# Which element-wise steps stand behind a read-out, and which engine takes the last unit's two subtractions, in the recurrence of a hybrid attention block

## The chip, the cores and the metric

The kernel runs on one core of a Trainium2 chip. The metric is the device time of one execution in microseconds; where several runs are given, their median. One further execution was profiled, and every duration below is from that profile or its trace.

## The reference

One block of a network on a sequence of 1024 positions with width 1024: a normalised and modulated input goes through one large projection `w_in`; its columns feed three things, an attention with a forget gate, a recurrence with a state for each of 8 heads, and two sigmoid gates that mix both results. A convolutional feed-forward part follows. What matters here is the recurrence:

```python
def step(state, inp):
    r_t, w_t, k_t, v_t, a_t, b_t = inp
    sa = jnp.einsum('bhvk,bhk->bhv', state, a_t)
    state = state * w_t[:, :, None, :] + sa[..., None] * b_t[:, :, None, :] + v_t[..., None] * k_t[:, :, None, :]
    y_t = jnp.einsum('bhvk,bhk->bhv', state, r_t)
    return state, y_t
...
mean = jnp.mean(y, axis=-1, keepdims=True)
var = jnp.mean(jnp.square(y - mean), axis=-1, keepdims=True)
y = ((y - mean) * lax.rsqrt(var + GN_EPS)).reshape(bsz, seq, RWKV_WIDTH) * ln_w + ln_b
```

It is computed in chunks of 64 positions, with matrices inside a chunk and a state handed from chunk to chunk.

## The kernel before, in words

**Stages.** Up to about 130 us come the modulation and the first projections; from about 140 to 610 us the recurrence; from 621 to 813 us the attention; after that the output projections and the feed-forward part, which is dense matrix work. All precise products are made from a higher half (`hi`, a rounded copy) and a lower half (`lo`, what the rounding left), in three passes.

**Units.** The recurrence works on eight units, numbered k = 0 to 7: four pairs of heads `p`, each in two halves `hf` of 512 positions. `pre(k, p, hf)` prepares a unit and `main(k, p, hf)` runs it. In `pre`, element-wise steps on VectorE (DVE) make the operands `ar` and `bk` and the product `rkb` (lines 780 to 792 of the kernel before); the matmuls `p` then multiply `bk` and `ar`, and their results are read into `E`. From `E` a triangular system goes through memory (`sm`, then `M`) and is solved on DVE by 31 pairs of small steps, `t` (line 828) and `E` (line 832); the result goes back through memory (`se`, then `TT`) to be used in `main` of that unit. The solving steps of one unit and the element-wise steps of the next are mixed in DVE's queue.

**The end of a unit.** `main` ends with a normalisation of `y` within each head. Its two sums over a head, `mu` and `va`, are made on TensorE (PE) by `head_sums`: ScalarE (ACT) rounds the input to a higher half (`Ztr`, `Zts`), GpSimd (POOL) subtracts to get the lower half (`Wtr`, `Wts`, line 735), and after a planned pause of 3400 ns two matmuls sum both halves.

**What fills PE.** Between the small matmuls of the recurrence, PE works through a queue of projection items: `ps_rkv` (inputs of later units), `v` (the values of the attention, in 16 pieces), and `gt` (gates). Each item fills one of two banks of the pool `pb` ("big"); it must be read out by ACT and DVE before the item after the next can begin in that bank. The read-out of `ps_rkv` is DVE line 410, that of `v` is line 1002 (`vs`). Both call `evac_done`.

**What sets the order.** PE's order is written by a planner (`Weave`): it adds up an estimate `weave.now` in ns for each matmul, and a chain that yields a number is taken up again when `weave.now` has moved on by it; until then PE gets projection items. DVE's, ACT's and POOL's order in this stage is made by a scheduler from the program and from added order dependences (`add_manual_dep`, without a semaphore). One such rule is the list `soft`: `evac_done(i)` puts each step in the list behind the read-out `i`, if the step was written less than 3000 planned ns before, and in the kernel before then empties the list.

**After the last unit.** `load_head(0)` and `load_head(1)` bring the attention's operands of the first two heads into `stA`, `stB` and `vh` by DMAs from POOL's queue; the attention's first matmuls are named `lg`.

Of the kernel before, what the change touches and what calls it, by code (L numbers as in the profile page):

```python
# [12 lines left out]
ALU = mybir.AluOpType  # L13
# [121 lines left out]
def hybrid_block(ctx: ExitStack, tc: tile.TileContext, a, out):  # L135
    nc = tc.nc
    weave = Weave()
    ctx.enter_context(tc.manual_schedule(engines={mybir.EngineType.PE}))

    def mm(o, lhsT, rhs, start, stop, more=False):  # L140

        weave.mm_cost(o, lhsT, rhs)
        nc.tensor.matmul(o, lhsT, rhs, start=start, stop=stop, skip_group_check=more)  # L143
# [5 lines left out]
    def f32(ap):  # L149
        return ap.bitcast(F32)  # L150

    tt, stt, ts = nc.vector.tensor_tensor, nc.vector.scalar_tensor_tensor, nc.vector.tensor_scalar
# [15 lines left out]
    def V(name, i=0, n=1):  # L168
        o, _ = VEC[name]
        return vec[:, o + i : o + i + n]  # L170
# [16 lines left out]
    nw0, na0, nkk, oka = (quads[:, 4 * x : 4 * x + 4] for x in range(4))  # L187
# [64 lines left out]
    soft = []  # L252

    def evac_done(i):
        for x, t in soft:
            if weave.now - t < 3000:
                tc.add_manual_dep(x.ins, i.ins.name, NOSYNC)
        soft.clear()
        return i
    first_step = []  # L260

# [8 lines left out]
    def behind_state(i):  # L270
        if marks.get("chain"):
            held.append(i)
        else:
            behind(i, "S")
# [112 lines left out]
    with ExitStack() as es:  # L387
# [7 lines left out]
        def gen(name):  # L395
            return pr.tile([128, NH], F32, tag="gen", name=name)

        def shifted(w, ti, hf, dst, prev, name, by_kt=False):

            ps = big(f"ps_{name}{hf}")  # L400
            yield from gemm_steps(ps, w, u, slice(hf * NH, hf * NH + NH), by_kt=by_kt)
            sh = shp.tile([128, NH + 1], F32, tag="sh", name=f"sh_{name}{hf}")
            if hf == 0:
                nc.vector.memset(sh[:, 0:1], 0.0)
            else:
                nc.vector.tensor_copy(sh[:, 0:1], prev)
            nc.scalar.activation(sh[:, 1 : NH + 1], ps, AF.Copy, scale=V("mu", ti))
            if hf == 0:
                nc.gpsimd.tensor_copy(prev, sh[:, NH : NH + 1])
            marks["bank"] = evac_done(stt(dst, ps, omu[:, ti : ti + 1], sh[:, 0:NH], op0=ALU.mult, op1=ALU.add))  # L410
# [16 lines left out]
        def qk_steps(w, i):  # L427
            sc_ = 0.125 if i < 4 else 1.0
            for hf in range(2):
                cs = slice(hf * NH, hf * NH + NH)  # L430
                ps = big(f"qk{i}_{hf}")
                yield from gemm_steps(ps, w, u, cs)
                hi = gsp.tile([128, NH], F32R, tag="sp0", name=f"qh{i}_{hf}")
                nc.scalar.activation(hi, ps, AF.Copy, scale=sc_)
                lo = gsp.tile([128, NH], F32R, tag="sp0", name=f"ql{i}_{hf}")
                evac_done(stt(lo, ps, sc_, f32(hi), op0=ALU.mult, op1=ALU.subtract))
                h0 = 2 * (i % 4)
                for t, k, r0 in ((hi, 0, 0), (lo, 0, 64), (hi, 2, 0)) if i < 4 else ((hi, 1, 0), (hi, 1, 64), (lo, 3, 0)):
                    for h in range(2):
                        nc.sync.dma_start(f32(d_st[h0 + h, k, r0 : r0 + 64, cs]), f32(t[h * 64 : h * 64 + 64, :]))  # L440
# [13 lines left out]
        with tc.tile_pool(name="st", bufs=1) as st, tc.tile_pool(name="stp", bufs=2, space=PS) as stp, \  # L454
# [126 lines left out]
            for half in range(2):  # L581
                for kt in u_steps(half):
                    low_part(kt, half, (0, 1))
                    if half == 0 and kt in (3, 5):
                        raw, hi, lo = low_raw[kt == 5]
# [13 lines left out]
        with tc.tile_pool(name="lg", bufs=1, reuse_waits="tile") as lg, \  # L599
# [46 lines left out]
            last = []  # L646
# [68 lines left out]
        def c3(ap):  # L715
            return ap.rearrange("p (c s) -> p c s", s=CH)
# [10 lines left out]
        Mt = rw.tile([128, NCU, 128], F32, name="Mt")  # L727
        nc.gpsimd.memset(Mt, 0.0)

        def head_sums(ps, x, hi, lo, behind_it=False):  # L730

            i = nc.scalar.copy(hi, x)
            if behind_it:
                behind_state(i)
            nc.gpsimd.tensor_tensor(lo, x, f32(hi), op=ALU.subtract)
            yield 3400
            mm(ps, blk_r, hi, start=True, stop=False)
            mm(ps, blk_r, lo, start=False, stop=True)

        def pre(k, p, hf):  # L740
# [3 lines left out]
            rr, kk, vv = rkv[p, hf]  # L744

            def tmp(nm, w=NH, bufs=1, dt=F32):
                return rw.tile([128, w], dt, tag=nm, name=f"{nm}{n}", bufs=bufs)

            def chunk_tile(nm, bufs, *dims):
                return rw.tile([128, *dims], F32, tag=nm, name=f"{nm}{n}", bufs=bufs)  # L750
# [3 lines left out]
            al = tmp("al")  # L754
            nc.sync.dma_start(al, d_lora[1, p, :, cs])
            for c0 in (0, 256):
                i = nc.vector.tensor_tensor_scan(cum[:, c0 : c0 + 256], cst2[:, 128:384], cum[:, c0 : c0 + 256], initial=0.0,
                                                 op0=ALU.mult, op1=ALU.add)
# [4 lines left out]
            en = tmp("en")  # L763
# [4 lines left out]
            yield 1275 if p + hf else 6000  # L768
            ssq = gen(f"ssq{n}")
            yield from head_sums(ssq, ksq, parts[:, 0, :], parts[:, 1, :])  # L770
            rn = tmp("ksq")
            nc.scalar.activation(rn, ssq, AF.Ln, bias=epsr[:, 2:3])
            nc.scalar.activation(rn, rn, AF.Exp, scale=-0.5)
            kr = tmp("kr")
            stt(kr, rn, 1e12, kk, op0=ALU.min, op1=ALU.mult)
            bk = chunk_tile("bk", 1, NCU, 3, CH)
# [1 line left out]
                yield 200  # L778
            ar = chunk_tile("ar", 2, 2, NCU, CH)
            stt(ar[:, 0], c3(kr), nkk[:, p : p + 1], el[:, :, 0:CH], op0=ALU.mult, op1=ALU.mult)  # L780
            stt(kr, kr, V("k_k", p), al, op0=ALU.mult, op1=ALU.mult)
            tt(bk[:, :, 0, :], c3(kr), c3(en), op=ALU.mult)
            nc.gpsimd.tensor_copy(bk[64:128, :, 2, :], bk[64:128, :, 0, :])
            tt(ar[:, 1], c3(rr), el[:, :, 1:], op=ALU.mult)
            soft.clear()
            soft.append((ts(al, al, V("k_a", p), oka[:, p : p + 1], op0=ALU.mult, op1=ALU.add), weave.now))
            soft.append((tt(al, al, kk, op=ALU.mult), weave.now))
            soft.append((tt(bk[:, :, 1, :], c3(al), c3(en), op=ALU.mult), weave.now))
            pcd = chunk_tile("pcd", 3, NCU)
            nc.gpsimd.tensor_copy(pcd, el[:, :, CH])  # L790
            rkb = tmp("ksq")
            stt(rkb, rr, V("r_k", p), al, op0=ALU.mult, op1=ALU.mult)
            yield 10500


# [5 lines left out]
            for c0 in range(0, NCU, 4):  # L801
                ps = [gen(f"p1_{n}{h}{c0}") for h in range(2)]
# [22 lines left out]
            for s in range(31):  # L825
                J, W = s // 4 + 1, 31 - s
                tv = t32[:, 0 : J * W].rearrange("p (j w) -> p j w", w=W)
                i = tt(tv, E32[:, 0:J, s : s + 1].to_broadcast([128, J, W]),  # L828
                       M32[:, s : s + 1, s + 1 : 32].to_broadcast([128, J, W]), op=ALU.mult)
# [29 lines left out]
            ps = [gen(f"tb{n}{h}") for h in range(2)]  # L859
# [17 lines left out]
        def main(k, p, hf):  # L877
# [10 lines left out]
            for h in range(2):  # L888
                i = nc.vector.transpose(X[B0[h], :, :], TT[B0[h], :, 0:32])
# [19 lines left out]
            Wt = rw.tile([128, NCU, CH], F32, tag="Wt", name=f"Wt{n}", bufs=1)  # L909
            for c0 in range(0, NCU, 4):  # L910
                ps = gen(f"uw{n}{c0}")
                for c in range(c0, c0 + 4):
                    for h in range(2):
                        x = (c - c0) * 128
# [6 lines left out]
            Zt = rw.tile([128, NCU, CH], F32, tag="Zt", name=f"Zt{n}", bufs=1)  # L921
            for c0 in range(0, NCU, 4):
                ps = gen(f"mz{n}{c0}")
                for c in range(c0, c0 + 4):
                    for h in range(2):
                        x = (c - c0) * 128
# [34 lines left out]
            y = rw.tile([128, NH], F32, tag="y", name=f"y{n}", bufs=1)  # L961
            nc.scalar.copy(y, yp.rearrange("p c s -> p (c s)"))

            def part(nm, i):
                return rw.tile([128, NH], F32R, tag=nm, name=f"{nm}{i}{n}", bufs=1)

            mu = gen(f"mu{n}")
            yield 700
            yield from head_sums(mu, y, part("Zt", "r"), part("Wt", "r"))
            stt(y, mu, -1.0 / CH, y, op0=ALU.mult, op1=ALU.add)  # L970
            ysq = rw.tile([128, NH], F32, tag="ysq", name=f"ysq{n}", bufs=1)
            nc.scalar.activation(ysq, y, AF.Square)
            yield 2700
            va = gen(f"va{n}")
            yield from head_sums(va, ysq, part("Zt", "s"), part("Wt", "s"))
            gg = rw.tile([128, NH], F32, tag="ysq", name=f"gg{n}", bufs=1)
            nc.sync.dma_start(gg, d_lora[2, p, :, cs])
            rs = rw.tile([128, NH], F32, tag="Zt", name=f"rs{n}", bufs=1)
# [268 lines left out]
    def bank(k, name):  # L1247
        return pb.tile([128, NH], F32, tag="big", name=name) if k > 5 else pz.tile([128, NH], F32, tag=f"p{k}", name=name)
# [48 lines left out]
    if "rest" in marks:  # L1297
        g, m = (gsp.tile([128, NH], F32, tag="sp0", name=f"rest{k}") for k in range(2))
        i = nc.scalar.activation(g, marks["rest"], AF.Abs)
# [33 lines left out]
    last = {}  # L1333
# [58 lines left out]
    for x in range(2):  # L1392
        for n in range(8):
            if x or n:
                k = 8 * x + n + 1
# [13 lines left out]
            if x == 1:  # L1409
                wo_load(n)  # L1410
                if n == 0:
                    lo = [hp.tile([128, NH], F32R, tag=tag, name=f"mgl0_{k}", bufs=bufs)
                          for k, (tag, bufs) in enumerate(5 * [("xq", 5)] + 2 * [("s", 2)] + [("dg", 1)])]
# [311 lines left out]
    ps = {t: [bank(k, f"wo{t}_{c}") for c, k in enumerate(ks)] for t, ks in enumerate(((0, 5), (6, 7), (1, 2)))}  # L1725
# [13 lines left out]
    def wo_do(t, k):  # L1739
        ps = [bank(k + c, f"wo{t}_{c}") for c in range(2)]  # L1740
        for kt in range(KT):
            wo_mm(t, kt, ps)
        return ps

    ps = wo_do(3, 3)
# [7 lines left out]
    ps = wo_do(4, 0)  # L1753
# [15 lines left out]
    for t, k in ((5, 2), (6, 6), (7, 4)):  # L1769
        ps = wo_do(t, k)  # L1770
# [244 lines left out]
    for s, k in enumerate(ORDER):  # L2015
        ps = banks[4:] if k in (7, 4, 2) else banks[0:4]
# [21 lines left out]
        for tp in range(4):  # L2038
            r = ssq[:, 16 + tp : 17 + tp]
# [86 lines left out]
```

## Time and profile before

| | |
|---|---|
| median of 3 runs | 1635.21 us (1632.43 to 1638.53) |
| profiled execution, its own time | 1634.44 us |
| its span | 1632.7 us |
| PE busy, share of the span | 1598.9 us, 98% |
| DVE busy | 1211.9 us, 74% |
| ACT busy | 827.9 us, 51% |
| POOL busy | 155.5 us, 10% |
| TensorE clock granted | 0.996 of full speed |

The profile's times are counted from the start of the span. A row of its timeline has a start, a duration, the engine, the line of the kernel, what is written from what, the shape and a count; in square brackets stands how long the engine had been idle before it, and what ended that. A run of equal instructions stands in one row. A busy PE is not PE at its peak, since matmuls overlap; a row's duration holds the first start to the last end.

### The profile page before, as it was taken

The numbers are of one execution on the slowest core, as the hardware profiler recorded it, in microseconds if no ns is written. First come the engines' busy times: TensorE is split into PE (matmuls) and PEld (weight loads), VectorE is DVE, ScalarE is ACT, GpSimd is POOL, SyncE is SP. The second block draws the span as 40 slices with busy tenths as digits, with TensorE's granted clock in tenths as the row PEclk, the third lists the DMA queues.
The fourth block names the chain that finished last, engine by engine and source line by source line (L and its number), as shares of the span: only waits on it lengthen the run. The fifth ranks groups of instructions, "written<-read, shape, count | busy, mean of one in ns | idle before, by whom it ended". The sixth has DMA issues, their size and how long they took to land.

```text
span 1632.7 us, 25956 instructions
## 1 busy us (share of the span) xinstructions
PE 1598.9 (98%) x9678; PEld 1334.0 (82%) x9678; DVE 1211.9 (74%) x2343; ACT 827.9 (51%) x1557; POOL 155.5 (10%) x189
## 2 busy tenths in 40 slices
PE   7899999999999999999999999999999999999998
PEld 7777878888978788888888888888888888888886
DVE  4786787878876526878669548987777777886677
ACT  5563344544455656778623235644444444555455
POOL 0011111112111011333122000000000000000000
PEclk9999999999999999999999999999999999999999
DMA  9397645543333336434197511233322322675363
GB/s 341 120 337 206 178 132 148 136 117 93 112 106 95 98 126 161 130 108 123 49 345 277 189 70 39 78 129 102 118 97 97 110 98 97 237 246 162 123 213 110
DMA packets 123543, 238.79 MB, mean 146 GB/s; under 512 B 42189, under 2 KB 51285, under 8 KB 123417
## 3 DMA queue, kind: packets, MB, share of 16 engines
q1 hardware_dynamic: 114936, 218.77, 41.1%
q0 software_dynamic: 8480, 18.37, 4.2%
q8 instruction: 76, 1.25, 0.3%
q14 instruction: 51, 0.41, 0.1%
HBM read 172.57 MB, written 64.50 MB: 145 GB/s over the span
## 4 chain that ended last, share of the span: by engine, by line
PE 70%; DVE 7%; DMA 2%; ACT 2%; issue 2%; SPq 1%; POOL 0%; DVEq 0%; POOLq 0%; ACTq 0%
PE X L143 15%; PE D L143 13%; PE Y L143 7%; PE wo L143 5%; PE br L143 5%; PE gt L143 5%; PE W L143 4%; PE ps_rkv L143 3%; PE rk_ps L143 3%; PE ov L143 2%; PE lg L143 2%; PE tp L147 1%; DMA stB<-d_st 1%; DVE E L832 1%; DVE t L828 1%
## 5 line engine op out<-in xcount | busy, mean ns | idle before, releaser
L143 PE MATMUL D<-op,op 128*128 128x512 f32 x924 | 209.8, 389 | 0.0
L143 PEld LDWEIGHTS D<-op,op 128*128 128x128 f32 x924 | 173.3, 188 | 36.3 <-DVE op L1327 0.3
L143 PE MATMUL X<-T_m,S 128*128 128x512 f32 x440 | 107.1, 390 | 0.0
L143 PEld LDWEIGHTS X<-T_m,S 128*128 128x128 f32 x440 | 82.5, 188 | 17.7 <-ACT T_m L1809 0.5
L1326 ACT CAST op<-g 128x512 fp32r<-128x512 f32 x77 | 47.8, 621 | 72.9 <-PE D L143 47.6
L1327 DVE TENSOR_TENSOR op<-g,op 128x512 fp32r<-128x512 f32 x77 | 53.0, 689 | 41.2 <-ACT op L1326 41.2
L1588 DVE SCALAR_TENSOR_TENSOR c<-ab,vec,c 128x512 f32<-128x512 f32 x88 | 65.8, 750 | 18.4 <-ACT c L1591 16.8
L828 DVE TENSOR_TENSOR t<-E,M 128x60 f32<-128x60 f32 (+24 forms) x248 | 55.5, 224 | 24.3 <-DMA M<-sm 17.6
L1554 DVE TENSOR_TENSOR A<-ur,A 128x512 fp32r<-128x512 f32 x64 | 44.0, 689 | 38.3 <-ACT A L1550 38.2
L1554 DVE TENSOR_TENSOR S<-ur,S 128x512 fp32r<-128x512 f32 x66 | 45.5, 691 | 35.2 <-ACT S L1550 35.1
L1550 ACT CAST S<-ur 128x512 fp32r<-128x512 f32 x66 | 41.1, 622 | 57.3 <-DVE ur L1543 30.4
L311 DVE TENSOR_TENSOR lo_in<-raw_in,hi_in 128x512 fp32r<-128x512 f32 x84 | 57.6, 725 | 16.0 <-PE gt L143 4.8
L143 PE MATMUL Y<-T_h,A 128*128 128x512 f32 x264 | 63.4, 389 | 0.0
L143 PE MATMUL Y<-T_h,S 128*128 128x512 f32 x264 | 63.3, 389 | 0.0
L1140 DVE TENSOR_TENSOR tl<-tp,th 128x512 fp32r<-128x512 f32 (+1 forms) x80 | 50.0, 631 | 15.3 <-ACT th L1137 14.9
L1550 ACT CAST A<-ur 128x512 fp32r<-128x512 f32 x64 | 39.6, 621 | 42.9 <-PE X L143 31.3
L832 DVE TENSOR_TENSOR E<-E,t 128x60 f32<-128x60 f32 (+24 forms) x248 | 56.6, 228 | 6.3
L309 ACT CAST hi_in<-raw_in 128x1024 fp32r<-128x1024 f32 x42 | 43.8, 1048 | 33.3 <-PE qk L143 13.9
L143 PE MATMUL W<-B_f,A 128*128 128x512 f32 x252 | 60.6, 389 | 0.0
L143 PE MATMUL X<-B_b,A 128*128 128x512 f32 x252 | 60.5, 389 | 0.0
L143 PEld LDWEIGHTS Y<-T_h,S 128*128 128x128 f32 x264 | 49.6, 188 | 10.3
L143 PEld LDWEIGHTS Y<-T_h,A 128*128 128x128 f32 x264 | 49.6, 188 | 10.3
(499 smaller groups left out, 4137.7 us busy)
## 6 DMA issues: line engine op xcount, KB each, us to landing
raw_in<-in_w_in SPq DMA_DIRECT2D x50, 512.0 KB
wm<-in_w_mod SPq DMA_DIRECT2D x48, 512.0 KB
ur<-in_w_up SPq DMA_DIRECT2D x44, 512.0 KB
g<-d_g SPq DMA_DIRECT2D x35, 512.0 KB
d_g<-gs SPq DMA_DIRECT2D x44, 256.0 KB
d_g<-c SPq DMA_DIRECT2D x33, 256.0 KB
d_st<-qh SPq DMA_DIRECT2D x64, 128.0 KB
stA<-d_st POOLq DMA_DIRECT2D x8, 1024.0 KB, 8.2
```

The source lines that it names most:

```text
L143: nc.tensor.matmul(o, lhsT, rhs, start=start, stop=stop, skip_group_check=more)
L147: nc.tensor.transpose(o, i, eye)
L309: nc.scalar.copy(hi, raw)
L311: nc.vector.tensor_tensor(lo[:, c : c + NH], raw[:, c : c + NH], f32(hi[:, c : c + NH]), op=ALU.subtract)
L828: i = tt(tv, E32[:, 0:J, s : s + 1].to_broadcast([128, J, W]), M32[:, s : s + 1, s + 1 : 32].to_broadcast([128, J, W]), op=ALU.mult)
L832: tt(E32[:, 0:J, s + 1 : 32], E32[:, 0:J, s + 1 : 32], tv, op=ALU.add)
L1140: tt(tl[:, 0:w], tp[:, 0:w], f32(th[:, 0:w]), op=ALU.subtract)
L1326: nc.scalar.copy(hi, src)
L1327: tt(lo, src, f32(hi), op=ALU.subtract)
L1550: nc.scalar.copy(hi, src)
L1554: tt(lo, src, f32(hi), op=ALU.subtract)
L1588: stt(c, ab[:, x + hf * NH : x + hf * NH + NH], V("conv_w", 22 * x + i), c, op0=ALU.mult, op1=ALU.add)
```

## The change

In `pre`, the list `soft` is emptied earlier, and six element-wise steps are put in it (`easy`) instead of three: besides the three that make `al` and the second part of `bk`, the scaling of `kr`, the first part of `bk`, and `rkb`. `evac_done` no longer empties the list, so that every read-out within 3000 planned ns goes ahead of the six, not the first alone. In `main` of the last unit (k = 7) both lower halves of the normalisation are subtracted on VectorE, the pause ahead of each pair of sums is 2300 ns instead of 3400, and the one ahead of the second sum is 1200 instead of 2700. POOL's queue after the last unit thus begins with the head loads.

```diff
--- before.py
+++ after.py
@@ -255,7 +255,6 @@
         for x, t in soft:
             if weave.now - t < 3000:
                 tc.add_manual_dep(x.ins, i.ins.name, NOSYNC)
-        soft.clear()
         return i
     first_step = []
 
@@ -727,13 +726,13 @@
         Mt = rw.tile([128, NCU, 128], F32, name="Mt")
         nc.gpsimd.memset(Mt, 0.0)
 
-        def head_sums(ps, x, hi, lo, behind_it=False):
+        def head_sums(ps, x, hi, lo, behind_it=False, last=False):
 
             i = nc.scalar.copy(hi, x)
             if behind_it:
                 behind_state(i)
-            nc.gpsimd.tensor_tensor(lo, x, f32(hi), op=ALU.subtract)
-            yield 3400
+            (nc.vector if last else nc.gpsimd).tensor_tensor(lo, x, f32(hi), op=ALU.subtract)
+            yield 2300 if last else 3400
             mm(ps, blk_r, hi, start=True, stop=False)
             mm(ps, blk_r, lo, start=False, stop=True)
 
@@ -778,18 +777,22 @@
                 yield 200
             ar = chunk_tile("ar", 2, 2, NCU, CH)
             stt(ar[:, 0], c3(kr), nkk[:, p : p + 1], el[:, :, 0:CH], op0=ALU.mult, op1=ALU.mult)
-            stt(kr, kr, V("k_k", p), al, op0=ALU.mult, op1=ALU.mult)
-            tt(bk[:, :, 0, :], c3(kr), c3(en), op=ALU.mult)
+            soft.clear()
+
+            def easy(i):
+                soft.append((i, weave.now))
+
+            easy(stt(kr, kr, V("k_k", p), al, op0=ALU.mult, op1=ALU.mult))
+            easy(tt(bk[:, :, 0, :], c3(kr), c3(en), op=ALU.mult))
             nc.gpsimd.tensor_copy(bk[64:128, :, 2, :], bk[64:128, :, 0, :])
             tt(ar[:, 1], c3(rr), el[:, :, 1:], op=ALU.mult)
-            soft.clear()
-            soft.append((ts(al, al, V("k_a", p), oka[:, p : p + 1], op0=ALU.mult, op1=ALU.add), weave.now))
-            soft.append((tt(al, al, kk, op=ALU.mult), weave.now))
-            soft.append((tt(bk[:, :, 1, :], c3(al), c3(en), op=ALU.mult), weave.now))
+            easy(ts(al, al, V("k_a", p), oka[:, p : p + 1], op0=ALU.mult, op1=ALU.add))
+            easy(tt(al, al, kk, op=ALU.mult))
+            easy(tt(bk[:, :, 1, :], c3(al), c3(en), op=ALU.mult))
             pcd = chunk_tile("pcd", 3, NCU)
             nc.gpsimd.tensor_copy(pcd, el[:, :, CH])
             rkb = tmp("ksq")
-            stt(rkb, rr, V("r_k", p), al, op0=ALU.mult, op1=ALU.mult)
+            easy(stt(rkb, rr, V("r_k", p), al, op0=ALU.mult, op1=ALU.mult))
             yield 10500
 
 
@@ -966,13 +969,13 @@
 
             mu = gen(f"mu{n}")
             yield 700
-            yield from head_sums(mu, y, part("Zt", "r"), part("Wt", "r"))
+            yield from head_sums(mu, y, part("Zt", "r"), part("Wt", "r"), last=k == 7)
             stt(y, mu, -1.0 / CH, y, op0=ALU.mult, op1=ALU.add)
             ysq = rw.tile([128, NH], F32, tag="ysq", name=f"ysq{n}", bufs=1)
             nc.scalar.activation(ysq, y, AF.Square)
-            yield 2700
+            yield 1200 if k == 7 else 2700
             va = gen(f"va{n}")
-            yield from head_sums(va, ysq, part("Zt", "s"), part("Wt", "s"))
+            yield from head_sums(va, ysq, part("Zt", "s"), part("Wt", "s"), last=k == 7)
             gg = rw.tile([128, NH], F32, tag="ysq", name=f"gg{n}", bufs=1)
             nc.sync.dma_start(gg, d_lora[2, p, :, cs])
             rs = rw.tile([128, NH], F32, tag="Zt", name=f"rs{n}", bufs=1)
```

## The prediction

> **What bounds the kernel now.** I read the page first, for the engines' shares.
>
> ```profile
> span 1632.7 us, 25956 instructions
> PE 1598.9 (98%) x9678; PEld 1334.0 (82%) x9678; DVE 1211.9 (74%) x2343; ACT 827.9 (51%) x1557; POOL 155.5 (10%) x189
> L1327 DVE TENSOR_TENSOR op<-g,op 128x512 fp32r<-128x512 f32 x77 | 53.0, 689 | 41.2 <-ACT op L1326 41.2
> ```
>
> PE is the bound, and work on other engines costs time only where PE stands. The change touches the stretch from 240 to 622 us, so the second view is that of PE's waits from 200 to 640 us (what waited, for what; total, times, longest):
>
> ```profile
> PE v L143 <- DVE vs L1002: 1.6, 2, 1.1
> PE va L143 <- POOL Wts L735: 0.9, 1, 0.9
> PE mu L143 <- POOL Wtr L735: 0.9, 1, 0.9
> PE sp L143 <- ACT S L950: 0.6, 1, 0.6
> PE zi L143 <- ACT X L899: 0.6, 1, 0.6
> PE ps_rkv L143 <- DVE k L410: 0.6, 1, 0.6
> PE va L143 <- ACT Zts L732: 0.6, 1, 0.6
> PE lg L143 <- DMA stB<-d_st: 0.3, 1, 0.3
> ```
>
> These nine stops sum to 6.1 us. An idle time is counted from the modelled end of the last matmul. The next could have started earlier: below, eight matmuls from 603.31 end with a start at 605.13, so they follow each other every 0.227 us, while one row of a single matmul is 0.39 long. So a stop costs some 0.16 more than its idle time, and all nine some 7.5 us, 0.46% of the time. That is the ceiling of this stretch. A measurement of this kernel can tell about 0.5% (8.2 us) from no change. Four of the stops are ones that the change aims at: the three on read-outs (`vs` twice, `k` once) and the one on `stB`.
>
> **The change, part one: the six steps go behind read-outs.** The unchanged rows of the instruction order show that only three units move: k = 2, 4 and 6. Unit 2, on DVE, where `E_1` and `t_1` are the solving steps of unit 1, `k_2108` is the read-out, and the rest are unit 2's steps and one weight's lower half; before:
>
> ```order
> L828 TENSOR_TENSOR t_1_1927<-E_1_1925,M_1_1920 128x35
> L781 SCALAR_TENSOR_TENSOR kr_0_2172<-kr_0_2172,vec,al_0_2130 128x512
> L832 TENSOR_TENSOR E_1_1925<-E_1_1925,t_1_1927 128x7x5
> L311 TENSOR_TENSOR lo_in_2397<-raw_in_2394,hi_in_2396 128x512 x2
> L782 TENSOR_TENSOR bk_0_2174<-kr_0_2172,en_0_2137 128x8x64
> L828 TENSOR_TENSOR t_1_1927<-E_1_1925,M_1_1920 128x28
> L410 SCALAR_TENSOR_TENSOR k_2108<-ps_rkv_2268,omu,sh_rkv_2390 128x512
> ```
>
> and now, in the same place:
>
> ```order
> L831 TENSOR_TENSOR t_1_1927<-E_1_1925,M_1_1920 128x35
> L835 TENSOR_TENSOR E_1_1925<-E_1_1925,t_1_1927 128x7x5
> L831 TENSOR_TENSOR t_1_1927<-E_1_1925,M_1_1920 128x28
> L310 TENSOR_TENSOR lo_in_2397<-raw_in_2394,hi_in_2396 128x512 x2
> L835 TENSOR_TENSOR E_1_1925<-E_1_1925,t_1_1927 128x7x4
> L409 SCALAR_TENSOR_TENSOR k_2108<-ps_rkv_2268,omu,sh_rkv_2390 128x512
> L785 SCALAR_TENSOR_TENSOR kr_0_2172<-kr_0_2172,vec,al_0_2130 128x512
> ```
>
> Two steps, `kr` and the first `bk`, went behind the read-out, and one small solving step went ahead of it. The trace there, ACT, DVE and PE:
>
> ```profile
> 238.72 0.69 ACT L407 ACTIVATE sh_rkv<-ps_rkv,vec 128x512 f32<-128x512 f32 x1 [0.45 <-PE ps_rkv L143]
> ...
> 244.20 0.75 DVE L410 SCALAR_TENSOR_TENSOR k<-ps_rkv,omu,sh_rkv 128x512 f32<-128x512 f32 x1
> ...
> 246.19 0.69 DVE L788 TENSOR_TENSOR bk<-al,en 128x512 f32<-128x512 f32 x1
> ...
> 245.00 0.73 PE L143 MATMUL ps_rkv<-u_hi,hi_in 128*128 128x512 f32 x2 [0.61 <-DVE k L410]
> 250.67 1.16 PE L143 MATMUL p<-ar,bk 64*128 64x128 f32 x16
> ```
>
> The read-out's input was there from 239.4 and DVE came to it at 244.20. Without two steps of some 0.7 (the rows above) and with one small step of about 0.2 more ahead, it starts about 1.0 earlier and is over by 244.0. PE wanted the bank at 245.00 - 0.61 - 0.16 = 244.23. So the whole stop goes: **-0.77 us**. What it costs: `bk`, whose last part is over at 246.9, comes perhaps 0.5 later. PE wants it at 250.67, now 249.9, so some 2.5 us of cover are left; nothing is paid.
>
> Unit 4 and unit 6, the same with `vs`:
>
> ```profile
> 337.13 0.38 ACT L1001 CAST vs<-v 128x256 fp32r<-128x256 f32 x1 [2.86 <-PE v L143]
> ...
> 340.19 0.42 DVE L1002 TENSOR_TENSOR vs<-v,vs 128x256 fp32r<-128x256 f32 x1
> ...
> 340.67 0.98 PE L143 MATMUL v<-hi_v,u_hi 128*128 128x256 f32 x6 [0.48 <-DVE vs L1002]
> ...
> 436.40 1.21 PE L143 MATMUL v<-hi_v,u_hi 128*128 128x256 f32 x8 [1.11 <-DVE vs L1002]
> ```
>
> In unit 4 all six steps (some 4 us) leave the front of the read-out and seven more small steps (1.6 us) come ahead of it, so it starts near 338 and PE doesn't stand: 0.48 + 0.16 = **-0.64 us**. In unit 6 two steps of some 0.7 go out of the read-out's way and three small ones of 0.25 come in: it starts at least 0.6 earlier, or up to 1.2 with the gaps between dependent steps, so of 1.11 + 0.16 = 1.27 between nothing and 0.7 remains.
>
> **Does a gain reach the end?** A stop that goes is lost again where PE next waits for something that didn't move. The chain of work that ended last tells (start, duration, what):
>
> ```profile
> 340.19 0.44 DVE vs L1002
> ...
> 435.92 0.42 DVE vs L1002
> ...
> 444.67 0.17 DVE t L828
> ...
> 447.33 1.16 DVE t L828
> ...
> 448.83 0.93 DVE E L832
> ...
> 468.02 0.69 PE zi L143 x30
> ```
>
> From unit 6's read-out at 435.92 on the chain lies on DVE, not on PE: DVE is full, the solving of unit 5 ends at 449.8, its result goes through memory (`se`, `TT`), and PE waits for what hangs on it. POOL, DVE and PE there, and ahead of them the first solving step of unit 2 on DVE:
>
> ```profile
> 266.01 0.79 DVE L828 TENSOR_TENSOR t<-E,M 128x31 f32<-128x31 f32 x1 [3.60 <-DMA M<-sm]
> ...
> 446.87 1.60 POOL L735 TENSOR_TENSOR al<-ksq,kr 128x512 fp32r<-128x512 f32 x1 [11.59 <-PE yp L143]
> ...
> 456.49 0.43 DVE L889 STREAM_TRANSPOSE X<-TT 32x256 f32<-32x256 f32 x1 [3.20 <-DMA TT<-se]
> ...
> 461.33 0.50 PE L143 MATMUL va<-Wts,blk_r 128*128 128x512 f32 x1 [0.86 <-POOL Wts L735]
> ```
>
> The change leaves the same instructions ahead of that last solving step, only in another order, so the end of the chain doesn't move by it. PE comes 0.6 to 1.2 us earlier to `va` and waits as much longer. Unit 6's gain is worth **0**. Unit 2's and unit 4's gains lie ahead of it. In unit 2, PE's `p` matmuls start a read-out and a transfer, and DVE stood idle for 3.60 until that transfer let the solving begin (266.01); so the solving moves with PE. In unit 4 the read-out at 340.19 is itself a link of the chain, and hands it to PE. So these two shift what follows, and stay.
>
> What can change that chain is POOL. While POOL subtracts (446.87 to 448.47), a `t` step that otherwise takes 0.17 took over 1.1, and ended when POOL did; the `E` step at 448.83 likewise beside the next subtraction. Together they lost some 1.7. POOL follows PE, and will come up to 1.2 earlier against DVE. The steps it meets then may be read-outs of `p`, which weren't held (nothing lost, -1.7), or all be such ones as are held (two subtractions of 1.3 to 1.6 in full, 2.9, +1.2). I take 0, the same two hits, and keep both ends.
>
> The Trainium skill, in "SBUF — State Buffer", section "Who interferes with whom", says that a VectorE instruction with two SBUF inputs and a GpSimd instruction that reads SBUF exclude each other for a whole instruction. The `t` row agrees (0.17 against over 1.1). By the rule, a read-out from PSUM with one SBUF input is never held, so the three moved read-outs come on time; the sum by the rule and by the rows is the same there.
>
> **Part two: the last unit.** PE's rows, where `gt` is a gate and `mu` and `va` are the two sums; before:
>
> ```order
> L143 MATMUL mu_1_6729<-Wtr_1_6743,blk_r 128x512
> L143 MATMUL gt_1_6738<-u_hi,lo_in_6532 128x512 x5
> L143 MATMUL gt_0_6786<-u_hi,hi_in_6673 128x512 x8
> L143 MATMUL gt_0_6786<-u_lo,hi_in_6673 128x512 x8
> L143 MATMUL gt_0_6786<-u_hi,lo_in_6674 128x512 x8
> L143 MATMUL va_1_6795<-Zts_1_6796,blk_r 128x512
> L143 MATMUL va_1_6795<-Wts_1_6797,blk_r 128x512
> ```
>
> and now:
>
> ```order
> L143 MATMUL mu_1_6729<-Wtr_1_6743,blk_r 128x512
> L143 MATMUL gt_1_6738<-u_lo,hi_in_6531 128x512 x2
> L143 MATMUL gt_1_6738<-u_hi,lo_in_6532 128x512 x8
> L143 MATMUL gt_0_6791<-u_hi,hi_in_6673 128x512 x7
> L143 MATMUL va_1_6768<-Zts_1_6769,blk_r 128x512
> L143 MATMUL va_1_6768<-Wts_1_6770,blk_r 128x512
> ```
>
> `mu` stands five gate matmuls earlier, and only 17 instead of 29 lie between it and `va`. The trace, ACT, DVE, POOL, PE, and one row of the chain:
>
> ```profile
> 591.00 0.31 ACT L950 ACTIVATE S<-sp,pcd 128x64 f32<-128x64 f32 x1 [0.77 <-PE sp L143]
> ...
> 599.94 1.29 DVE L311 TENSOR_TENSOR lo_in<-raw_in,hi_in 128x512 fp32r<-128x512 f32 x2 [0.51 <-PE gt L143]
> ...
> 601.17 1.30 POOL L735 TENSOR_TENSOR Wts<-ysq,Zts 128x512 fp32r<-128x512 f32 x1 [4.62 <-ACT Zts L732]
> ...
> 603.14 1.00 POOL L1045 DMA_DIRECT2D stB<-d_st  x1
> 610.45 0.70 POOL L1043 DMA_DIRECT2D stA<-d_st  x1
> ...
> 598.08 0.40 PE L143 MATMUL mu<-Ztr,blk_r 128*128 128x512 f32 x1
> ...
> 603.31 1.98 PE L143 MATMUL gt<-u_hi,lo_in 128*128 128x512 f32 x8
> 605.13 0.40 PE L143 MATMUL va<-Zts,blk_r 128*128 128x512 f32 x1
> ...
> 621.52 0.50 PE L143 MATMUL lg<-stB 68*128 68x512 f32 x1 [0.34 <-DMA stB<-d_st]
> ...
> 603.14 18.33 DMA stB<-d_st
> ```
>
> PE comes to `mu` at 598.08 - 5 x 0.227 = 596.9 and to the second `va` at 596.9 + 2 x 0.227 + 17 x 0.227 + 0.23 = 601.4 to 601.5. On DVE, `Wts` now stands behind the pair `lo_in`, which waits until PE has released its buffer at 599.9 and ends at 601.2. No row shows a subtraction of this kind on DVE; the nearest, `op` with one PSUM input, is 0.69, and POOL's own is 1.30. So `Wts` is there at 601.9 (602.5 by the other), and PE stands **+0.4 us** (0 if `lo_in` runs behind it, 1.0 by the longer). The 0.69 is the nearer row, as the same engine on the same size.
>
> Head loads: nothing of the normalisation is left in POOL's queue, so the first load waits for the last `S` of ACT, over at 591.3, instead of POOL's `Wts` at 602.4. `stB` is issued at 592, and even with its 18.33 lands at 610.4. PE comes to this `lg` at 621.52 - 0.5 - 1.4 + 0.4 = 620.0. The stop goes: 0.34 + 0.16 = **-0.5 us**. The loads of head 1 follow at once; before, they stood at 610.45, behind a cast that waits for PE. Nothing else is in POOL's queue there, and of the six issues the longest shown takes 1.00, so they are over long before that cast.
>
> Sum: -0.77 - 0.64 + 0 + 0.4 - 0.5 = **-1.5 us**, from 1634.4 to 1632.9 in the profiled execution's own time. The median of the runs lies 0.8 above that execution, so I forecast a median of 1633.7.
>
> **The rivals.**
> *Unit 6's gain stays too.* POOL's hits fall away and the chain on DVE ends 1.7 earlier; PE, which has up to 1.2 more to wait there and its old stops besides, follows it in full. For it: POOL moves against DVE. Against: DVE's instructions stay the same set, and something is held wherever POOL works beside small steps. It gives -1.5 - 1.7 = -3.2, a median of 1632.0. Chance 0.2.
> *Nothing arrives.* The gains of units 2 and 4 too are swallowed by chains that didn't move (PE's wait for POOL at `mu`, in the second view, is an old stop that could take them in), and 0.4 against 0.5 remains from the last unit: -0.1, or +1.1 with POOL's full hits, medians of 1635.1 to 1636.3. Chance 0.15.
> *The head loads starve each other.* Slower: with both heads' loads issued in one go, `stB` of head 0 shares the engines with head 1's. In the trace the loads of head 1 were issued at 610.45, 7.3 us behind it. If each of the two ran at half speed from the start, `stB` would land at 592.1 + 2 x 18.33 = 628.8, and `lg` would stand 8.8 us: 8.8 - 1.5 = +7.3, a median of 1642.5. It decides from a landing later than 620.0, 27.9 us after the issue, and each us beyond costs one us. Against it: packets of one queue are mostly taken in order, as far as `stB` behind `stA` shows. Chance 0.05.
>
> **How the numbers follow.** Forecast 0.6, rivals 0.2, 0.15 and 0.05. The first three lie between -3.2 and +1.1, medians of 1632.0 to 1636.3. The runs before scatter by -2.8 and +3.3 about their median; a median of three scatters by about half of that, which I add at both ends, rounded outwards: 1630 to 1638. Faster by over 0.5% needs more than the ceiling of 7.5 us, so it is left to a cause that I don't see, 0.04; slower by over 0.5% is the third rival a little beyond its price or an unseen cause, 0.05; 0.91 remains.
>
> **What would show it.** Right: no stop of `ps_rkv` on `k` near 244 nor of `v` on `vs`; longer stops of `va` and `zi` near 458 to 466; a stop of 0.4 at the last `va`; `stA` issued near 590, `lg` without a stop, and all that follows 1 to 2 us earlier. Wrong: stops of `p` on `bk` near 249, 346 or 441, or `lg` waiting for `stB`.

## The result, and the profile after

| | before | changed |
|---|---|---|
| median of the runs | 1633.80 us (6 runs, 1632.38 to 1638.53) | 1643.65 us (6 runs, 1640.33 to 1645.11) |
| ratio | 1 | 1.0055, 95% interval 1.0039 to 1.0071 |
| profiled execution, its span, mean granted clock | 1634.44 us, 1632.7 us, 0.996 | 1645.11 us, 1643.3 us, 0.992 |

The changed kernel is some 9 us slower (0.55% of 1634, interval 6 to 12 us). The forecast was 1633.7 us in a range of 1630 to 1638, so it was wrong in sign and the time lies outside the range. The engines' shares tell next to nothing of it; the page after:

```profile
span 1643.3 us, 25950 instructions
PE 1603.5 (98%) x9678; PEld 1335.2 (81%) x9678; DVE 1213.3 (74%) x2345; ACT 827.7 (50%) x1557; POOL 153.8 (9%) x187
```

PE is busy 4.6 us longer for the same 9678 matmuls, and stands about 6 us longer. Where it stands is in the view of PE's waits from 200 to 640 us (total, times, longest):

```profile
PE rk_ps L143 <- DVE gs L379: 4.7, 1, 4.7
PE va L143 <- ACT Zts L731: 1.8, 1, 1.8
...
PE mu L143 <- ACT Ztr L731: 0.6, 1, 0.6
PE va L143 <- DVE Wts L734: 0.2, 1, 0.2
```

The four stops that the change aimed at, on `k`, on `vs` (twice) and on `stB`, are gone, and the one on `zi`'s `X` with them. The first line is new, and larger than everything that went. It belongs to the projection behind the last gate matmuls (`rk_ps`), which needs a PSUM bank that the gate's read-out `gs` on DVE has to empty. The timeline around it, DVE, PE and POOL:

```profile
606.64 0.75 DVE L985 SCALAR_TENSOR_TENSOR y<-y,vec,bon 128x512 f32<-128x512 f32 x1
617.11 0.69 DVE L986 TENSOR_TENSOR gg<-y,gg 128x512 f32<-128x512 f32 x1 [9.72 <-DMA gg<-d_lora]
617.72 0.68 DVE L379 SCALAR_TENSOR_TENSOR gs<-gt,gs 128x512 f32<-128x512 f32 x1
...
618.46 3.78 PE L143 MATMUL rk_ps<-u_hi,hi_in 128*128 128x512 f32 x8 [4.69 <-DVE gs L379]
622.04 3.15 PE L143 MATMUL rk_ps<-u_lo,hi_in 128*128 128x512 f32 x8
...
593.64 0.73 POOL L1046 DMA_DIRECT2D stA<-d_st  x1 [39.96 <-ACT S L953]
...
597.62 0.56 POOL L1050 DMA_DIRECT2D vh<-d_v  x1
```

Read it from the bottom. POOL, free of the lower halves, issues all six head loads (4.26 MB) from 593.64 on, 8.8 us earlier than before. DVE has its `y` ready at 607.4 and comes to the product with the gate vector `gg`, whose 256 KB are loaded on SP's queue. It stands 9.72 us for them. Behind it in DVE's queue is `gs`, whose input was there from about 610.3, and PE stands 4.69 us for `gs`. Then PE's first sixteen matmuls take 3.78 and 3.15 us for eight, where eight take 2.00 otherwise. The same places before, SP's issue of `gg`, DVE and PE:

```profile
602.49 0.32 SPq L977 DMA_DIRECT2D gg<-d_lora  x1
...
608.81 0.69 DVE L983 TENSOR_TENSOR gg<-y,gg 128x512 f32<-128x512 f32 x1
609.42 0.68 DVE L380 SCALAR_TENSOR_TENSOR gs<-gt,gs 128x512 f32<-128x512 f32 x1
...
611.04 1.98 PE L143 MATMUL rk_ps<-u_hi,hi_in 128*128 128x512 f32 x8
```

The chain of work that ended last, after, goes through the load itself, and the windows from 590 to 630 us (busy time of PE, PEld, DVE, ACT, POOL; then granted clock, DMA share, GB/s) show the collision and what PE lost. The DMA share is the time that packets took as a share of 16 engines, and can exceed 1:

```profile
603.90 13.14 DMA gg<-d_lora
...
617.11 0.69 DVE gg L986
...
618.46 8.58 PE rk_ps L143 x24
```

```profile
600.00:610.00 10.00, 9.78 (x44) 7.73 (x43) 4.42 (x7) 7.38 (x12) 0.00 (x0) 1.00 1.22 254
610.00:620.00 10.00, 5.31 (x21) 4.05 (x20) 1.29 (x2) 1.82 (x4) 1.04 (x1) 0.88 0.64 190
620.00:630.00 10.00, 10.00 (x36) 8.04 (x35) 1.33 (x3) 3.71 (x7) 0.00 (x0) 0.78 0.14 51
```

Before, in the first two of these windows:

```profile
600.00:610.00 10.00, 10.00 (x46) 8.27 (x45) 4.63 (x7) 5.96 (x11) 4.08 (x5) 1.00 0.75 232
610.00:620.00 10.00, 10.00 (x46) 8.29 (x45) 1.81 (x4) 5.66 (x10) 2.70 (x4) 1.00 1.21 252
```

`gg` takes 13.14 us from issue to the semaphore; the DMA share is 1.22 in the stretch in which it is issued (0.75 before, where the like crowd came only when `gg` was there), and the granted clock falls to 0.88 and 0.78 behind PE's stop. So the theory to be tested was: **theory 1, the early head loads make `gg` late, and DVE's queue hands that to PE**. Against it stood that the reordered steps cost time (theory 2), that the lower halves on DVE and the shorter pauses cost time by themselves, and that the two parts only cost together. Two things had to be told apart besides: what of the head loads it is that delays `gg`, and whether the slow rate of PE comes from the stop.

### The profile page after: what moved, and what is told of

Read it like the earlier page. It is cut to its first block, busy times and chain, and to the rows that moved or that the text cites. A ratio compares the mean times of both kernels' runs of the same rounds, so it can differ in the third digit from the quotient of the medians.

```text
span 1643.3 us, 25950 instructions
## 1 busy us (share of the span) xinstructions
PE 1603.5 (98%) x9678; PEld 1335.2 (81%) x9678; DVE 1213.3 (74%) x2345; ACT 827.7 (50%) x1557; POOL 153.8 (9%) x187
## 4 chain that ended last, share of the span: by engine, by line
PE 58%; DVE 4%; DMA 4%; ACT 2%; issue 1%; SPq 0%; POOL 0%; DVEq 0%; ACTq 0%; POOLq 0%
PE X L143 15%; PE D L143 13%; PE Y L143 7%; PE wo L143 5%; PE W L143 4%; PE rk_ps L143 4%; PE gt L143 3%; PE ov L143 2%; PE lg L143 2%; PE tp L147 1%; PE br L143 1%; DMA wm<-in_w_mod 1%; DMA raw_wo<-in_w_o 1%; DMA gg<-d_lora 1%; DVE quads L1103 1%
```

## The experiments

All ratios are against the kernel before, run beside each kernel on the same chip.

**The kernel before, profiled again.**

> The kernel before, unchanged, with a second profile. Theory 1 (the 9.9 us come from the last unit's gate vector gg, which lands late among the head loads): the ratio is 1.000, and PE's stop on ql near 187, which is 2.1 us longer in the changed kernel's profile though nothing has moved there yet, differs from run to run by 1 to 2 us. Theory 2 (the reordered steps themselves cost some of it, from 180 us on): this stop stands where it stood before, within 0.3 us.

Ratio 0.9996 (0.9988 to 1.0005). The waits of PE from 150 to 200 us, this run's and the changed kernel's:

```profile
PE qk L143 <- DVE ql L436: 0.4, 1, 0.4
```

```profile
PE qk L143 <- DVE ql L435: 1.7, 1, 1.7
```

In the first profile of before this stop was absent; in the runs below it is 0.2 to 0.7. It varies from one execution to the next, though by less than the 1 to 2 us expected, and 1.7 is the largest seen. I count these 2.1 us (the place is at 185.69 before, at 187.80 in the changed kernel's profile) as belonging to that execution: the runs below that have the new order of the six steps show 0.2 to 0.6 there. One profile of the changed kernel can't exclude that it has a cause.

**Part one alone.** The edit: the changed kernel, with the last unit as before.

```
-            (nc.vector if last else nc.gpsimd).tensor_tensor(lo, x, f32(hi), op=ALU.subtract)
-            yield 2300 if last else 3400
+            nc.gpsimd.tensor_tensor(lo, x, f32(hi), op=ALU.subtract)
+            yield 3400
...
-            yield 1200 if k == 7 else 2700
+            yield 2700
```

> Only the six steps behind each near read-out; the last unit's lower halves stay on POOL with the long pauses. Theory 1: no cost, 1.5 us faster to equal (ratio 0.9990 to 1.0000), stops on k near 244 and on vs near 334 and 430 gone, gg lands within 6.5 us, no stop of 4.7 us on the gate read-out, PE at its usual spacing of 0.227 us. Theory 2 (reordering costs): 2 to 5 us slower (1.0012 to 1.0030), from the stops of va and mu at 308 and 460.

Ratio 0.9992 (0.9983 to 1.0001): theory 2 is out. PE's waits from 200 to 640 us:

```profile
PE va L143 <- ACT Zts L731: 2.0, 1, 2.0
...
PE mu L143 <- ACT Ztr L731: 0.4, 1, 0.4
```

The three read-out stops are gone here too, and `va` stands 1.4 longer (2.0 against 0.6 in the first profile of before, 0.9 against the 1.1 in the second), `mu` 0.4.

**Part two alone.** The edit is the other half of the diff, on the kernel before.

> Only the last unit's part: lower halves on VectorE, shorter pauses, head loads early; the six steps as before. Theory 1: nearly the whole loss, 8 to 11 us slower (1.0049 to 1.0067), gg lands 10 us or more after its issue, rk_ps waits 4 to 5 us for gs, and PE's rows behind it go at half rate. Theory 2: 5 to 8 us slower only. A third theory, that the two parts need each other: less than 3 us slower.

Median 1642.37 us, 7.7 above that of before; ratio 1.0039 (1.0025 to 1.0053, 4 to 9 us). DVE and PE:

```profile
616.23 0.69 DVE L983 TENSOR_TENSOR gg<-y,gg 128x512 f32<-128x512 f32 x1 [9.65 <-DMA gg<-d_lora]
...
617.58 3.30 PE L143 MATMUL rk_ps<-u_hi,hi_in 128*128 128x512 f32 x8 [4.62 <-DVE gs L380]
620.67 2.41 PE L143 MATMUL rk_ps<-u_lo,hi_in 128*128 128x512 f32 x8
```

The same stop, with the same cause: `gg` was issued at 603.09, 13.1 us ahead of its product. The ratio lies under the 1.0049 that I expected at least; its interval overlaps that range and the changed kernel's. The time alone would also fit theory 2's 5 to 8 us, which the run of part one has ruled out. The loss belongs to part two, and the parts don't need each other.

**The gate vector loaded early, the head loads as in the changed kernel.**

```
             passed.add((k, 0))
+            if k == 7:
+                gg = rw.tile([128, NH], F32, tag="cum", name=f"gg{n}", bufs=1)
+                nc.sync.dma_start(gg, d_lora[2, p, :, cs])
             yield 3400
```

(and the load at its old place only for k < 7)

> The changed kernel, but the last unit's gate vector gg is loaded some 50 us earlier, into a buffer of its own, so that it is there before the head loads begin; the head loads stay early. Theory 1: the stop of 4.7 us and the slow rate behind it go, and the time is that of the kernel before less 0 to 2 us (ratio to it 0.9988 to 1.0000). Rival A (the early head loads harm otherwise, by lg's own tiles or by the weights on SP): 3 us slower or more remain (1.0018 and above). Rival B (lower halves on VectorE and shorter pauses cost by themselves): the stop remains or is replaced by one on Wts of 2 us and more.

Ratio 0.9989 (0.9981 to 0.9998). POOL still issues the first head load at 591.57; DVE and PE:

```profile
605.35 0.69 DVE L990 TENSOR_TENSOR gg<-y,gg 128x512 f32<-128x512 f32 x1
...
611.53 1.98 PE L143 MATMUL rk_ps<-u_hi,hi_in 128*128 128x512 f32 x8
```

The product doesn't wait, the stop and the slow rate are gone, and with them the whole loss, while the head loads, the DVE halves and the short pauses stay. That refutes both rivals of this run: of PE's stops there only 0.2 on `Wts` is left.

**Nothing on DVE waits for the late vector.** This kernel leaves the gate out of the last unit, so its output is another.

```
-            tt(gg, y, gg, op=ALU.mult)
-            nc.sync.dma_start(d_orw[p, :, cs], gg)
+            if k == 7:
+                out = rw.tile([128, NH], F32, tag="cum", name=f"out{n}", bufs=1)
+                tt(out, y, bon, op=ALU.mult)
+                nc.sync.dma_start(d_orw[p, :, cs], out)
+            else:
+                tt(gg, y, gg, op=ALU.mult)
+                nc.sync.dma_start(d_orw[p, :, cs], gg)
```

> The changed kernel, with the loads as they are, gg's too; but the last unit's product leaves out the gate vector: it multiplies by bon, which is long there, and stores from another buffer, so that nothing on VectorE waits for gg. Theory 1 (the loss arises because the gate read-out gs stands behind the waiting product in VectorE's queue): gg still lands 10 us or more after its issue, yet the stop on gs and the slow rate go, and the time is that of the kernel before less 0 to 2 us (0.9988 to 1.0000). Rival (the loads crowd out something else, weights or memory ports): 3 us or more remain (1.0018 and above).

Ratio 1.0002 (0.9992 to 1.0012). The windows, and DVE:

```profile
600.00:610.00 10.00, 9.78 (x43) 7.78 (x42) 5.29 (x8) 6.26 (x11) 0.15 (x1) 1.00 1.21 275
610.00:620.00 10.00, 10.00 (x46) 8.29 (x45) 1.33 (x3) 4.73 (x8) 0.88 (x1) 1.00 0.56 179
```

```profile
608.15 0.69 DVE L379 SCALAR_TENSOR_TENSOR gs<-gt,gs 128x512 f32<-128x512 f32 x1 [2.20 <-ACT gs L378]
```

The transfers crowd as in the changed kernel (DMA share 1.21), `gg`'s among them, and PE runs through at a clock of 1.00. When `gg` landed can't be seen here, since nothing waits for it. So the crowd costs nothing by itself: it costs by the one DVE instruction that waits, and by `gs` behind it.

**What of the head loads delays `gg`.** First, the second lower half on POOL again, so that all six loads wait behind it:

```
-            (nc.vector if last else nc.gpsimd).tensor_tensor(lo, x, f32(hi), op=ALU.subtract)
+            (nc.vector if dve else nc.gpsimd).tensor_tensor(lo, x, f32(hi), op=ALU.subtract)
...
-            yield from head_sums(mu, y, part("Zt", "r"), part("Wt", "r"), last=k == 7)
+            yield from head_sums(mu, y, part("Zt", "r"), part("Wt", "r"), last=k == 7, dve=k == 7)
```

> The changed kernel, but the last unit's second lower half (Wts) is worked out on POOL again, so that all six head loads wait behind it until about 603 and are then issued together; gg's load keeps its place behind that. Theory 1a (what is queued on the DMA engines ahead of gg's issue decides): little is ahead of gg, it lands within 9 us, the stop on gs is under 1.5 us and the time within 3 us of the kernel before (0.999 to 1.002). Theory 1b (the amount of head loads in flight beside gg decides, whenever they began): 4.1 MB stand beside it, it lands 10 us or more after its issue, and the time is 6 to 10 us longer (1.0037 to 1.006).

Ratio 1.0023 (1.0012 to 1.0033), between the two. POOL's first load, SP's issue of `gg`, DVE and PE:

```profile
599.88 0.73 POOL L1046 DMA_DIRECT2D stA<-d_st  x1
...
600.98 0.38 SPq L980 DMA_DIRECT2D gg<-d_lora  x1
...
611.74 0.69 DVE L986 TENSOR_TENSOR gg<-y,gg 128x512 f32<-128x512 f32 x1 [8.29 <-DMA gg<-d_lora]
...
613.08 2.11 PE L143 MATMUL rk_ps<-u_hi,hi_in 128*128 128x512 f32 x8 [3.27 <-DVE gs L379]
```

Second, only head 1's three loads behind the first late cast, as before, and head 0's early:

```
+        held_by = marks.get("cast")
...
+        if h == 1 and held_by is not None:
+            for x in loads:
+                tc.add_manual_dep(x.ins, held_by.ins.name, NOSYNC)
```

> The changed kernel, but the three loads of head 1 stand behind the first late cast on POOL again (some 16 us later); those of head 0 stay early. Theory 1a: head 0's 2.1 MB, issued from 593 on, are nearly through when gg is issued at 604, so gg lands within 6 us, the stop is under 0.5 us and the time is that of the kernel before less 0 to 2 us (0.9988 to 1.0000). Theory 1b: half the loads, half the harm, 3 to 5 us longer (1.0018 to 1.003).

Ratio 0.9999 (0.9987 to 1.0011). SP, DVE and PE:

```profile
599.99 0.32 SPq L981 DMA_DIRECT2D gg<-d_lora  x1
...
608.37 1.32 DVE L987 TENSOR_TENSOR gg<-y,gg 128x512 f32<-128x512 f32 x1 [4.88 <-DMA gg<-d_lora]
...
610.34 2.12 PE L143 MATMUL rk_ps<-u_hi,hi_in 128*128 128x512 f32 x8 [0.50 <-DVE gs L380]
```

From its issue to the product that waits for it, `gg` took 8.4 us with head 0's loads begun 10 us ahead of it (589.74), 10.8 with all six issued around it, and 13.2 with all six begun 10 us ahead; 6.8 in the second profile of before, where the first load began 0.1 us ahead:

```profile
601.53 0.32 SPq L977 DMA_DIRECT2D gg<-d_lora  x1
...
608.33 0.69 DVE L983 TENSOR_TENSOR gg<-y,gg 128x512 f32<-128x512 f32 x1 [0.58 <-DMA gg<-d_lora]
```

Neither theory's numbers hold. 1a expected under 9 in the first edit and 6 in the second; 1b had the landing of the first edit right (10 or more), but not its time, and expected half the loss in the second, where there is none. In direction 1a does better: the amount beside it is largest where all six begin around it, yet the longest landing is where they began earliest, with all of them issued ahead of it.

What stood ahead of `gg` can be told from the bytes of each queue in the changed kernel's trace. SP's queue there:

```profile
599.77 0.32 SPq L382 DMA_DIRECT2D d_gate<-gs  x1
603.34 0.33 SPq L296 DMA_DIRECT2D raw_in<-in_w_in  x1
603.90 0.32 SPq L980 DMA_DIRECT2D gg<-d_lora  x1
```

From 594 to 604 us POOL's queue moved 2.27 MB and SP's nothing, though a store of 256 KB had been issued on it at 599.77; in the second profile of before the like store, issued at 596.77, was through by 600. The run without the wait shows the same, 2.30 MB and nothing from 592 to 602, with such a store issued at 597.60. From 603.90 to 617.04 SP's queue moved 1.30 MB beside 1.82 of POOL's. So the early head loads held up SP's whole queue, and `gg` found that store and 512 KB of weights undone ahead of it. That is nearer to 1a than to 1b. Why SP's queue moved nothing stays open.

**The stop without any transfer moved.** Eight more products on DVE in the kernel before:

```
+            if k == 7:
+                more = rw.tile([128, NH], F32, tag="cum", name=f"more{n}", bufs=1)
+                for _ in range(8):
+                    tt(more, y, bon, op=ALU.mult)
             tt(gg, y, gg, op=ALU.mult)
```

> The kernel before with its loads untouched, and eight more VectorE products of y and bon (about 0.62 us apart, 4.9 us in all) between y and the gate read-out gs. Theory 1 with the clock as a consequence of the stop: PE stops for about 4.1 us at rk_ps (4.9 less some 0.8 of slack) and then runs 15 to 30 matmuls at 0.3 to 0.45 us instead of 0.227, so 5.5 to 7.5 us longer (1.0034 to 1.0046). If the slow rate comes from the crowd of transfers and not from the stop: the rows behind the stop keep 1.98 us for eight, and it is 3.8 to 4.4 us longer (1.0023 to 1.0027).

Median 1641.91 us, ratio 1.0041 (1.0026 to 1.0056). PE:

```profile
616.53 3.78 PE L143 MATMUL rk_ps<-u_hi,hi_in 128*128 128x512 f32 x8 [5.29 <-DVE gs L380]
620.11 2.85 PE L143 MATMUL rk_ps<-u_lo,hi_in 128*128 128x512 f32 x8
```

The loads are those of before, and the slow rate is there. So it comes with the stop, not with the early loads. (The stop is 1.2 longer than expected, as seven of the products took 5.88 together and not 4.3.) Its ratio lies in the range expected of the stop with its slow rate. How long a stop it takes, with five instead of eight:

> As the run with eight more VectorE products, but with five. The eight delayed gs by about 6.4 us and PE by 5.29, so these delay gs by some 4.0 and stop PE for 2.7 to 3.0 us. Theory 1c (the clock only falls after a stop of more than about 3.3 us, since the rows behind a stop of 3.27 us kept 2.11 us for eight and those behind 4.6 us and more did not): the rows behind it keep 2.0 to 2.1 us, and the time is 2.7 to 3.1 us longer (1.0016 to 1.0019). Rival (the slow rate grows with the stop, 0.5 us for each us of stop): rows of 2.5 us and more, 4.0 to 4.6 us longer (1.0024 to 1.0028).

Ratio 1.0021 (1.0011 to 1.0031).

```profile
613.66 3.19 PE L143 MATMUL rk_ps<-u_hi,hi_in 128*128 128x512 f32 x8 [3.12 <-DVE gs L380]
616.65 2.54 PE L143 MATMUL rk_ps<-u_lo,hi_in 128*128 128x512 f32 x8
```

A stop of 3.12 us is followed by 1.75 us of lost rate (3.19 - 2.00 + 2.54 - 1.98), while the one of 3.27 above lost 0.1. So theory 1c falls. The rival's rows came (2.5 and more), and its time lies within the interval; what speaks against it is the loss of 0.1 behind 3.27 us, where it would give 1.6. So the loss isn't set by the length of the stop alone (4.62 us: 1.7; 4.69: 2.95; 5.29: 2.65). The ten executions of the kernel with the second lower half on POOL point the same way. The profiled one, with the 3.27 and a granted clock of 0.996 over the span, is the fastest (1636.80 us); four at 0.992 and 0.993 took 1639.18 to 1642.01, the other six 1636.80 to 1638.60 at 0.994 to 0.996. How long PE stood in those without a profile isn't known.

**The early gate vector, once more.**

> The changed kernel with the last unit's gate vector loaded early, run again: the first measurement gave 0.9989 with an interval of 0.9981 to 0.9998. If it is really faster than the kernel before, 0.998 to 0.9995 again, by the gains of units 4 and 6 that nothing takes back; if it was chance, 0.9995 to 1.0005.

Ratio 0.9999 (0.9989 to 1.0008). The gain of the first measurement didn't come again, though the two intervals overlap: with the collision taken out, the changed kernel is as fast as the one before, and no version here is shown to beat it.

## Why the prediction was wrong

*The step that failed* is the paragraph on the head loads: "Nothing else is in POOL's queue there". I followed POOL's queue and the loads' own user (`lg`), and took the six loads as done with when they were issued. I didn't ask which other transfers are issued while they run. `gg` is, 10 us later, on SP's queue, and the trace of before had what was needed: the transfer took up to 6.3 us there (602.49 to 608.81), its DVE product came when it had hardly landed (in the second profile it waits 0.58), and `gs`, on which PE's next bank hangs, stands behind it. The step gave -0.5 us. It gave that -0.5 indeed (`lg` stands no more), and +4.85 for the stop (4.69 and 0.16 as in the prediction's rule) and +2.95 for the half rate behind it.

*The clock.* No step had it: every stop was priced at its own length, and the page before shows no stop of that length in the stretch. In the runs stops of 4.62 and 4.69 us cost 6.5 and 7.8, with the 0.16.

*The rival "The head loads starve each other"* had the right kind of mechanism, loads that share the engines, with a size of +7.3 that comes near. Its victim was wrong: `lg` waited for no tile at all. That its sum is near is chance.

*Part one, units 2 and 4* (-0.77 and -0.64, "these two shift what follows, and stay"): the stops went in full, but in this profile the gains didn't stay. PE in the changed kernel, near 310 and near 460:

```profile
309.22 0.50 PE L143 MATMUL mu<-Ztr,blk_r 128*128 128x512 f32 x1 [0.61 <-ACT Ztr L731]
...
461.41 0.50 PE L143 MATMUL va<-Zts,blk_r 128*128 128x512 f32 x1 [1.82 <-ACT Zts L731]
```

`mu`'s stop on `Ztr` is new, and takes back unit 2's 0.77; `va`'s grew from 0.6 to 1.82, and takes back much of unit 4's and unit 6's. Measured from the `qk` matmuls at 185.69 and 187.80, PE comes to the last `mu` after 412.4 us before and 411.2 in the changed kernel, and `mu` stands five matmuls (1.1 us) earlier: the balance of part one is -0.1. In these two profiles that is the rival "Nothing arrives". The other profiles lie nearer to the forecast. From the `qk` matmuls to the last `yp` matmuls, which stand a little ahead of the last `mu`, PE took 406.7 to 407.7 us in the five profiles with the old order of the steps (before, twice, part two alone, eight and five products more) and 404.7 to 407.1 in the seven with the new one, 1.0 less on the mean. `mu`'s stop on `Ztr` stands in three of these seven only (0.4 to 0.6), and `va`'s on `Zts` is 0.6 to 1.4 in the old order and 1.4 to 2.0 in the new. So part of the gain is taken back, and how much differs from execution to execution; the time of part one alone (0.9983 to 1.0001) can't tell -0.1 from -1.5.

*Unit 6* (stop gone or shortened, worth 0, given back at `va` and `zi`): right in the main. The stop went in full, and `va` took it; `zi`'s stop didn't grow. POOL's hits on DVE near 447 came out nearly as forecast, 2.2 against 1.9: a pair of lower halves lost 1.1 there and an `E` step 1.1 (2.37 and 1.26 us long), where a `t` and an `E` step had lost 1.9 together.

*The last unit's `va`*, +0.4 by `Wts` behind `lo_in` on DVE: `lo_in` runs from 601.97 to 603.26 and `Wts` 0.68 behind it, and the stop is 0.22 and 0.16, so 0.4. Right, and with the 0.69 that I took from the nearer row.

The sum for the profiled execution: +2.1 at `qk` (that execution's own), -0.1 for part one, +0.4 at `va`, +4.85, +2.95, -0.5 make 9.7 of the 9.8 by which PE is late when it begins the second `rk_ps` of the head (625.59 before, 635.36 now). At the end it is 10.7; the 0.9 that comes after wasn't followed. The medians differ by 9.9, the ratio says 9.0. Without the 2.1 the terms make 7.6, which lies in the ratio's 6 to 12.

## What to carry to other kernels

When a transfer is moved to begin earlier, list every other transfer that is issued until it has landed, on all queues, and see who stands behind each one's waiting instruction; its own reader may be the one that profits least. A load whose reader sits in the middle of a busy engine's queue should be issued so early that no crowd can reach it: a free buffer and one moved line took the whole loss back here. A gain at a stop has to be followed to the next wait of the same engine before it counts; in this kernel three stops went, and in the profile after the next two waits took nearly all of them.

## What the runs showed of the hardware

- A 256 KB load on SP's queue took 6.8, 8.4, 10.8 and 13.2 us from issue to its reader's start, by what was ahead of it and beside it. In the 13.14 us of the chain's row the engines moved 3.1 MB (238 GB/s), 1.30 on SP's queue and 1.82 on POOL's, and from 594 to 604 us 2.27 MB on POOL's and none on SP's. The Trainium skill, "DMA: Bandwidth & Descriptors", section "Queues, rings and completion order", says that each DMA engine takes turns between its queues, a packet at a time. With equal turns and packets of one size, `gg` and the 512 KB of weights issued 0.56 us ahead of it on the same queue would have had half of the 254 GB/s, some 6 us (an estimate by that page and the window's row). The trace doesn't agree: the wait was twice that, and a queue with 256 KB issued on it at 599.77 moved nothing until 604. Packet size doesn't tell it (4.26 MB in 1952 packets on POOL's queue, 2.39 MB in 1021 on SP's, from 590 to 620 us); the cause stays open.
- PE's half rate behind a stop: eight matmuls in 3.78 instead of 2.00 us. It cost 1.7 to 2.95 us behind stops of 3.12, 4.62, 4.69 and 5.29 us; behind stops of 3.27 and 0.50 only 0.1 was lost. The Trainium skill, "TensorE: Matmul & The Clock Gate", Part 1, "The HAM clock gate", says that the clock halves after an idle window of about 3.4 us and returns after a busy one, and that the window runs freely. The half rate agrees. That two stops of nearly one length fared differently would fit a window that runs freely; but the 3.12 us, 3.28 with the 0.16, are shorter than a whole such window, so the rule doesn't cover the half rate behind them. Where the windows lay no run here shows.
- Products on DVE with two SBUF inputs: one followed another at 0.61 us (608.78 and 609.39). Of the next seven the first took 1.52 us beside POOL's cast (609.49 to 610.97), and the others followed each other at 0.73 us, also when POOL's three issues were over at 613.18. They all write the same tile; what made 0.73 of 0.61 wasn't tried.
